# A decoder layer on one core: GpSimd adds before it reads back, pooling differences and norm splits issued sooner

## The chip, the cores and the metric

One NeuronCore of a Trainium2 chip runs the whole layer; nothing is exchanged with other cores. The metric is device time in microseconds. Engines are named as the profile names them: PE (TensorE), DVE (VectorE), ACT (ScalarE), POOL (GpSimd) and SP (SyncE). Each takes its instructions in program order and waits on semaphores. SP only issues transfers here; POOL computes and issues transfers from the same list.

## The reference, cut to what matters

All arrays are float32, with 256 tokens of width 1024. The part around the change is the first mixer and its norm:

```python
z = h @ w_in[l]                              # u | q | k | v, 512 columns each
pool_out = multiscale_pool(u, w_pool[l], pool_scale[l])
attn_out = moba_attention(q, k, v)           # 8 heads of 64; one block of 256, so causal softmax
mix = jnp.concatenate([pool_out, attn_out], axis=-1) @ w_out[l]
h = layer_norm(DEEPNORM_ALPHA * h + mix, ln1_g[l], ln1_b[l])
h = layer_norm(DEEPNORM_ALPHA * h + memory_cross_attention(h, mem, ...), ...)
h = layer_norm(DEEPNORM_ALPHA * h + swiglu(h, ...), ...)

# multiscale_pool, for the four groups g of 128 channels, windows w = 2, 4, 8, 16
groups.append((c_hi - c_lo) / count - uf[..., sl])   # trailing mean minus the token
mixed = einsum('bsgc,gcd->bsgd', pooled, w_pool)     # one 128x128 matrix for each group
```

## The kernel before, in words

Every large product is made of three float32r matmuls: each operand is split into a high part (a cast on ACT) and a low part (a subtraction on DVE), and PE adds high by high, high by low and low by high. The weights stream in through SP: `w12r` is piece number 12 as it lands, `w12h` and `w12l` its two parts. The splits of weight pieces are slipped into the program while PE works on earlier pieces, nine pieces ahead.

The program is written out by hand. Generators such as `do_u`, `do_xk` and `do_xv` yield after every few matmuls, and `run(u, 4)` advances one by four steps; what stands between two `run` calls is issued between those steps, on whichever engine it belongs to. The stages that matter here, in order:

- `do_u` projects u into `upad` in two chunks of 16 steps. When the first step of the second chunk is asked for, the first chunk is copied to `upad` by ACT (line 621) and `windows(0)` and `windows(1)` are issued: POOL adds shifted copies (line 593: one add for group 0, two for group 1, three for 2, four for 3) and corrects the first 16 tokens (line 595). At the end of the second chunk the same happens for groups 2 and 3.
- `scores` makes the softmax of four attention heads and one half of the tokens. `probs_out(hp)` turns two heads' probabilities on DVE (line 425, four 32x32 transposes a call) and sends them to HBM from POOL's queue (line 428, `pd<-ps`). `probs_in(hp)` reads them back transposed with four transfers from POOL's queue (line 436, `pt<-pd`), which wait until the transfer out has landed. `attend(hp)` is the product with v on PE (lines 581 and 582).
- `pool_diff(g)` is one DVE instruction (line 600) that subtracts the token from the window's mean, in `upad`. `mix_pool(g)` is the group's product on PE (line 604), with its split on ACT and DVE (lines 605 and 606).
- `do_xk` projects the memory's keys for the cross-attention in 64 steps, as PE's work between all this. Then comes the mix with w_out, norm 1, and `do_xv` (values of the memory) as PE's work while norm 1's result `h1` goes to HBM and back through SP's queue (`hr<-hd`).
- `h1_split(t)` splits half t of the result that came back, `hr`, into `h1Th` on ACT and `h1Tl` on DVE (lines 404 and 405). The projection `do_xq`, which follows `do_xv` on PE, reads both, and `xscores` reads its result `xq`.

Of the kernel before, what the change touches and what calls it, by code (L numbers as in the profile page):

```python
# [42 lines left out]
class Stream:  # L43
# [114 lines left out]
    def next(self):  # L158

        i = len(self.tiles)  # L160
        return i + (2 if i < len(self.items) and self.items[i][0] == "sums" else 1)
# [28 lines left out]
def decoder_layer(  # L190
# [105 lines left out]
    def split_mem(k):  # L296
        split(mT[0][:, k:k + 4, :], mT[1][:, k:k + 4, :], mr[0][:, k:k + 4, :])
# [97 lines left out]
    def run(gen, n=None):  # L395

        while n is None or n > 0:
            if next(gen, gen) is gen:
                return False
            n = None if n is None else n - 1  # L400
        return True
# [18 lines left out]
    def turned(blocks, n, name, queue=nc.sync):  # L420

        st = sp.tile([P, 4, n, 32], F32, name=f"{name}s", tag="pair", bufs=3)
        for at, src in blocks:
            m = src.shape[1]
            nc.vector.transpose(st[:, :, at:at + m, :].rearrange("p j m b -> p m j b"),  # L425
                                src.rearrange("p m (j b) -> p m j b", b=32))
        via = hp.tile([P, 4, n * 32], F32, name=f"{name}d")
        queue.dma_start(via, st.rearrange("p j m b -> p j (m b)"))  # L428
        return via
# [101 lines left out]
    def scores(hq, t):  # L531
        w = (t + 1) * P
        pss = [bank(f"ps{j}").rearrange("p (h s) -> p h s", h=2) for j in range(2)]
        for h in range(2):
            for j in range(2):
                hs = slice(j * HD, (j + 1) * HD)
                hp = 2 * hq + h
                nc.tensor.matmul(pss[j][:, h, :w], qT[hs, hp, t * P:(t + 1) * P], kT[hs, hp, :w],
                                 start=True, stop=True)
        todo = []  # L540
        for j in range(2):
            pr = sp.tile([P, 2, S], F32, name="pr", bufs=PR_BUFS)[:, :, :w]
            mx = sp.tile([P, 2], F32, name="mx", bufs=6)
            for h in range(2):
                nc.vector.tensor_tensor_reduce(pr[:, h, :], pss[j][:, h, :w], tri[:, S - w:], -1.0, -NEG,  # L545
                                               op0=OP.add, op1=OP.min, accum_out=mx[:, h:h + 1])
            todo.append((pr, exps(pr, pr, mx, -1.0)))
            probs[hq, t, j] = pr
        for pr, sm in todo:
            scaled(pr, sm)  # L550
# [6 lines left out]
    def probs_out(hp):  # L557
        blocks = []
        for j in range(2):
            for t in range(T):  # L560
                pr = probs[hp // 2, t, j][:, hp % 2]
                blocks.append((3 * j + t, pr.rearrange("p (m c) -> p m c", c=P)))
        turns[hp] = turned(blocks, 6, "p", nc.gpsimd)

    def probs_in(hp):
        if hp % 2 == 0:
            homes[hp // 2] = ap.tile([P, 2, KD * P], F32, tag="a8", name=f"pt{hp // 2}")
        raw = homes[hp // 2][:, hp % 2, :4 * 6 * 32].rearrange("p (i m b) -> p i m b", i=4, m=6)
        raw = landed(turns[hp], 6, "p", nc.gpsimd, raw).rearrange("p i m b -> p m i b")
        pts[hp] = [(raw[:, 3 * j:3 * j + 2], raw[:, 3 * j + 2]) for j in range(2)]  # L570
# [3 lines left out]
    def attend(hp):  # L574
        po = bank("po")
        for j in range(2):
            hs = slice(j * HD, (j + 1) * HD)
            vs = slice((2 * hp + j) * HD, (2 * hp + j + 1) * HD)
            s0, s1 = pts[hp][j]
            out = po[hs, :S].rearrange("p (t i b) -> p t i b", t=T, i=4)  # L580
            nc.tensor.matmul(out, vt[:, 0, vs], s0, start=True, stop=False)
            nc.tensor.matmul(out[:, 1], vt[:, 1, vs], s1, start=False, stop=True)
        split(cT[0][:, 4 + hp, :], cT[1][:, 4 + hp, :], po[:, :S])
# [14 lines left out]
    def pool_diff(g):  # L598
        pl = upad[:, g, PADW:]
        nc.vector.scalar_tensor_tensor(pl, sums[g][:, PADW:], 1.0 / WINDOWS[g], pl, op0=OP.mult, op1=OP.subtract)  # L600

    def mix_pool(g):
        pm = bank("pm")
        nc.tensor.matmul(pm[:, :S], wpl[:, g, :], upad[:, g, PADW:], start=True, stop=True)
        nc.scalar.activation(cT[0][:, g, :], pm[:, :S], AF.Copy, bias=0.0, scale=psc[:, g:g + 1])
        nc.vector.scalar_tensor_tensor(cT[1][:, g, :], pm[:, :S], psc[:, g:g + 1],
                                       r32(cT[0][:, g, :]), op0=OP.mult, op1=OP.subtract)


    def do_v():  # L610
        pieces = [(t, 0, 512) for t in range(T)]
        acc = {piece: accbank("pv") for piece in pieces}
        yield from proj_rows(acc, c_v, lambda k: (xT[0][:, k], xT[1][:, k]), pieces, True, True, True)
        for piece in pieces:
            nc.scalar.copy(vt[:, piece[0], :], acc[piece])

    def do_u():
        for c in range(2):
            ps = accbank("pu").rearrange("p (f t) -> p f t", f=2)
            yield from proj_t([ps[:, f, :] for f in range(2)], c_u[c], xT)  # L620
            nc.scalar.copy(upad[:, 2 * c:2 * c + 2, PADW:], ps)
            for f in range(2):
                windows(2 * c + f)
# [3 lines left out]
    def do_xk():  # L627
        for c in range(4):
            ps = accbank("pxk").rearrange("p (f t) -> p f t", f=2)
            yield from proj_t([ps[:, f, :] for f in range(2)], c_xk[c], mT)  # L630
            split(xkT[0][:, 2 * c:2 * c + 2, :], xkT[1][:, 2 * c:2 * c + 2, :], ps)

    v, u, xk = do_v(), do_u(), do_xk()
# [8 lines left out]
    probs_out(1)  # L642
    run(u, 6)
    split_mem(0)
    run(u, 4)
    probs_in(0)
    probs_in(1)
    run(u, 6)
    split_mem(4)
    run(u)  # L650
    run(xk, 2)
# [3 lines left out]
    run(xk, 8)  # L655
    scores(1, 1)
    run(xk, 8)
    probs_out(2)
    probs_out(3)
    mix_pool(0)  # L660
    attend(0)
    run(xk, 6)
    mix_pool(1)
    pool_diff(2)
    probs_in(2)
    probs_in(3)
    run(xk, 8)
    attend(1)
    pool_diff(3)
    ws.pace = 2  # L670
    run(xk, 8)
    mix_pool(2)
# [94 lines left out]
    def h1_split(t):  # L767
        raw = turns1[t].rearrange("p i k b -> p k i b")
        for k0 in (0, 4):
            h, l = [h[:, k0:k0 + 4, t * P:(t + 1) * P].rearrange("p k (i b) -> p k i b", i=4) for h in h1T]  # L770
            split(h, l, raw[:, k0:k0 + 4])
# [23 lines left out]
    def do_xv():  # L795
        acc = {piece: (bank if piece == PIECES[3] else accbank)("xv") for piece in PIECES}
        yield from proj_rows(acc, c_xv, lambda k: (mT[0][:, k], mT[1][:, k]),
                             PIECES, True, True, True)
        for t, c0, c1 in PIECES:
            split(xv[0][:, t, c0:c1], xv[1][:, t, c0:c1], acc[t, c0, c1])  # L800

    gv = do_xv()
    run(gv, 7)
    h1_split(0)
    run(gv, 5)
    h1_split(1)
    run(gv)

# [430 lines left out]
```

## Time and profile before

| | us |
|---|---|
| median of three runs | 372.5 |
| lowest and highest of them | 371.69 and 373.01 |
| the profiled execution, whole time | 372.51 |
| its span, from the first to the last instruction | 370.7 |

The profiled execution stands at the median, and 1.81 us of it lie outside the span. The granted TensorE clock is 0.998 of full speed over the span. In the rows below a start is in us from the span's start; the second number of a timeline row is its duration, and what stands in brackets is the idle time of that engine just before the row with what ended it.

### The profile page before, as it was taken

How to read it: one execution, taken by the hardware profiler on the slowest of the kernel's cores; microseconds unless marked ns; L12 is line 12 of the kernel's file. 1: busy time of each engine (PE TensorE's matmuls, PEld its weight loads, DVE VectorE, ACT ScalarE, POOL GpSimd, SP SyncE). 2: the span in 40 equal slices, each digit the busy share in tenths (PEclk: the TensorE clock that was granted, in tenths of full speed). 3: DMA queues.
4: the chain of work that ended last, by engine and by line, in shares of the span. 5: the costliest groups of instructions: out<-in, count | busy, mean ns of one | idle time of the engine just before them, and what ended most of it. 6: DMA issues, size and time to landing. Idle time of an engine off the chain costs nothing.

```text
span 370.7 us, 5690 instructions
## 1 busy us (share of the span) xinstructions
PE 362.7 (98%) x2007; PEld 312.7 (84%) x2007; DVE 301.6 (81%) x449; ACT 193.3 (52%) x289; POOL 59.2 (16%) x94
## 2 busy tenths in 40 slices
PE   8999999999999999999999999999999999999994
PEld 8997998897888899988878888888888888888882
DVE  5777898984599797765889897999999995789864
ACT  5656865753253565554229363754655555577000
POOL 1000059140020003320100042402321400000010
PEclk9999999999999999999999999999999999999999
DMA  7997599799615996846106998669887977758011
GB/s 244 416 422 286 187 338 303 272 280 362 214 66 173 357 356 234 277 149 207 57 2 191 400 273 262 212 204 361 271 290 254 315 260 245 232 166 260 9 57 58
DMA packets 33550, 88.21 MB, mean 238 GB/s; under 512 B 4209, under 2 KB 12401, under 8 KB 33393
## 3 DMA queue, kind: packets, MB, share of 16 engines
q1 hardware_dynamic: 31232, 82.66, 65.1%
q0 software_dynamic: 1712, 4.72, 4.0%
q10 hardware_dynamic: 576, 0.46, 0.4%
q8 instruction: 16, 0.26, 0.3%
q14 instruction: 14, 0.11, 0.1%
HBM read 80.48 MB, written 7.34 MB: 237 GB/s over the span
## 4 chain that ended last, share of the span: by engine, by line
PE 71%; issue 13%; DVE 6%; DMA 4%; POOL 3%; ACT 1%; SPq 0%; DVEq 0%; POOLq 0%; ACTq 0%
PE pg L343 10%; PE pg L342 10%; PE pg L341 10%; PE pqk L477 6%; PE acc L341 5%; PE acc L342 5%; PE acc L343 5%; PE pxk L359 2%; PE x L342 2%; PE x L343 2%; PE x L341 2%; PE acc L1121 1%; PE acc L1122 1%; PE acc L1120 1%; DMA pd<-ps 1%
## 5 line engine op out<-in xcount | busy, mean ns | idle before, releaser
L708 POOL TENSOR_TENSOR rs<-rs,mhalf 128x1 f32<-128x1 f32 x6 | 5.5, 910 | 128.2 <-DVE rs L707 128.2
L939 POOL TENSOR_TENSOR sraw<-gr 128x128 f32<-128x128 f32 x7 | 7.1, 1018 | 76.7 <-DMA gr<-gd 63.4
L1181 ACT ACTIVATE diag<-ident,rs 128x128 f32<-128x128 f32 x1 | 0.4, 402 | 22.0 <-POOL rs L708 22.0
L514 ACT ACTIVATE pr<-pr,mx 128x128 f32<-128x128 f32 (+1 forms) x16 | 7.1, 446 | 8.6 <-DVE mx L545 8.6
L919 ACT ACTIVATE sg<-pg 128x256 f32<-128x256 f32 x22 | 8.2, 381 | 6.4 <-PE pg L343 6.3
L428 POOL DMA_DIRECT2D pd<-ps x4 | 2.4, 612 | 48.5 <-DVE ps L425 48.2
L436 POOL DMA_DIRECT2D pt<-pd x16 | 8.8, 555 | 6.9 <-DMA pd<-ps 4.2
L920 DVE TENSOR_TENSOR sg<-sg,pg 128x256 f32<-128x256 f32 x22 | 8.6, 415 | 1.2 <-ACT sg L919 0.9
L404 ACT CAST h2Th<-tp 128x512 fp32r<-128x512 f32 x4 | 2.4, 588 | 13.5 <-PE tp L415 13.4
L405 DVE TENSOR_TENSOR gTl<-gr,gTh 128x512 fp32r<-128x512 f32 x11 | 8.0, 731 | 0.5 <-ACT gTh L404 0.5
L436 POOL DMA_DIRECT2D xr<-xd x12 | 6.5, 551 | 9.8 <-DMA xd<-xs 5.7
L404 ACT CAST gTh<-gr 128x512 fp32r<-128x512 f32 x11 | 6.8, 614 | 2.5 <-DMA gr<-gd 2.5
L514 ACT ACTIVATE xpr<-xs,mx 128x256 f32<-128x256 f32 x8 | 3.7, 471 | 8.1 <-DVE mx L525 8.1
L425 DVE STREAM_TRANSPOSE gs<-sg 128x512 f32<-128x512 f32 x11 | 7.7, 703 | 0.0
L428 POOL DMA_DIRECT2D xd<-xs x3 | 1.7, 576 | 33.8 <-DVE xs L425 33.8
L700 DVE BATCH_NORM_STATS2 st<-r 128x6 f32<-128x512 f32 (+1 forms) x10 | 6.4, 641 | 0.3
L940 POOL TENSOR_TENSOR sraw<-sraw,gr 128x128 f32<-128x128 f32 x7 | 6.5, 927 | 0.5
L519 DVE RECIPROCAL sm<-sm 128x2 f32<-128x2 f32 x12 | 2.0, 164 | 5.5 <-ACT xpr L514 4.4
L521 DVE TENSOR_SCALAR pr<-pr,sm 128x128 f32<-128x128 f32 (+1 forms) x16 | 6.2, 428 | 0.3
L713 DVE SCALAR_TENSOR_TENSOR r<-r,mv,g 128x512 f32<-128x512 f32 x9 | 6.4, 744 | 0.0
L941 POOL TENSOR_TENSOR sraw<-gr 128x128 f32<-128x128 f32 x7 | 6.1, 868 | 0.0
L719 DVE SCALAR_TENSOR_TENSOR h<-r,rs,b 128x512 f32<-128x512 f32 x8 | 5.6, 746 | 0.0
(1329 smaller groups left out, 1490.2 us busy)
## 6 DMA issues: line engine op xcount, KB each, us to landing
gd<-gs SPq DMA_DIRECT2D x11, 256.0 KB, 5.2
gr<-gd SPq DMA_DIRECT2D x44, 64.0 KB, 2.3
pd<-ps POOLq DMA_DIRECT2D x4, 384.0 KB, 4.5
pt<-pd POOLq DMA_DIRECT2D x16, 96.0 KB, 7.0
g<-in_ln_g SPq DMA_DIRECT2D x3, 512.0 KB, 5.8
b<-in_ln_b SPq DMA_DIRECT2D x3, 512.0 KB, 6.6
wr<-in_w_qkv SPq DMA_DIRECT2D x5, 256.0 KB, 4.6
mr<-in_mem_t SPq DMA_DIRECT2D x1, 1024.0 KB, 11.9
```

Source lines behind the costliest of these rows:

```text
L341: nc.tensor.matmul(ps, wa, ya, start=start, stop=False, skip_group_check=part)
L342: nc.tensor.matmul(ps, wa, yb, start=False, stop=False, skip_group_check=part)
L343: nc.tensor.matmul(ps, wb, ya, start=False, stop=stop, skip_group_check=part)
L359: nc.tensor.matmul(pss[f], w[:, s], y, start=k == 0 and f == 0 and n == 0, stop=k == KD - 1 and n == 2, skip_group_check=True)
L404: nc.scalar.copy(h, ps)
L405: nc.vector.tensor_sub(l, ps, r32(h))
L425: nc.vector.transpose(st[:, :, at:at + m, :].rearrange("p j m b -> p m j b"), src.rearrange("p m (j b) -> p m j b", b=32))
L436: queue.dma_start(raw[32 * j:32 * (j + 1)].rearrange("p i m b -> p i (m b)"), via[:, j, :].rearrange("(i a) r -> a i r", i=4))
L477: nc.tensor.matmul(qk[i][:, f, :], w[:, c * P:(c + 1) * P], y, start=k == 0 and f == 0 and w is hi and y is x_hi, stop=k == KD - 1 and w i ...
L514: nc.scalar.activation(dst[:, j, :], src[:, j, :], AF.Exp, bias=mx[:, j:j + 1], scale=sign, accum_out=sm[:, j:j + 1])
L919: nc.scalar.activation(sg, ps[:, :CW].rearrange("p (f b) -> p f b", f=2), AF.Silu, bias=0.0, scale=1.0)
L920: nc.vector.tensor_mul(sg, sg, ps[:, CW:].rearrange("p (f b) -> p f b", f=2))
```

## The change

Three things move; no instruction is added or taken away. First, `probs_in(0)` and `probs_in(1)` are issued after the first step of u's second chunk and no longer four steps ahead of the chunk's end, so that `windows(0)` and `windows(1)` stand ahead of them. Second, `pool_diff(2)` stands ahead of `probs_out(2)`, and `pool_diff(3)` where `pool_diff(2)` stood. Third, `h1_split(0)` comes after 6 steps of `do_xv` in place of 7, and `h1_split(1)` after 10 in place of 12.

```diff
     split_mem(0)
-    run(u, 4)
+    run(u, 10)
     probs_in(0)
     probs_in(1)
-    run(u, 6)
     split_mem(4)
...
     scores(1, 1)
     run(xk, 8)
+    pool_diff(2)
     probs_out(2)
     probs_out(3)
     mix_pool(0)
     attend(0)
     run(xk, 6)
     mix_pool(1)
-    pool_diff(2)
+    pool_diff(3)
     probs_in(2)
     probs_in(3)
     run(xk, 8)
     attend(1)
-    pool_diff(3)
...
     gv = do_xv()
-    run(gv, 7)
+    run(gv, 6)
     h1_split(0)
-    run(gv, 5)
+    run(gv, 4)
     h1_split(1)
     run(gv)
```

POOL's list from the transfer out of heads 0 to 3 (`pd<-ps`, one row for both) to the third group's sums, before:

```order
L428 DMA pd<-ps 128x768 x2
L436 DMA pt_641<-pd 32x4x192 x8
L593 TENSOR_TENSOR win<-upad 128x271
L595 TENSOR_TENSOR win<-win,fac 128x16
L593 TENSOR_TENSOR win<-upad 128x271
L593 TENSOR_TENSOR win<-win 128x269
L595 TENSOR_TENSOR win<-win,fac 128x16
L593 TENSOR_TENSOR win<-upad 128x271
```

The same stretch of POOL's list with the change:

```order
L428 DMA pd<-ps 128x768 x2
L593 TENSOR_TENSOR win<-upad 128x271
L595 TENSOR_TENSOR win<-win,fac 128x16
L593 TENSOR_TENSOR win<-upad 128x271
L593 TENSOR_TENSOR win<-win 128x269
L595 TENSOR_TENSOR win<-win,fac 128x16
L436 DMA pt_675<-pd 32x4x192 x8
L593 TENSOR_TENSOR win<-upad 128x271
```

The five instructions of groups 0 and 1 now stand ahead of the eight read-backs (four for heads 0 and 1, then four for heads 2 and 3).

On DVE, around the transposes of `probs_out(2)`, the difference of the third group (`upad<-win,upad`) comes in ahead of the first transpose:

```order
 L405 TENSOR_TENSOR xkTl<-pxk,xkTh 128x512
 L143 TENSOR_TENSOR w27l<-w27r,w27h 128x1024
+L600 SCALAR_TENSOR_TENSOR upad<-win,upad 128x256
 L425 STREAM_TRANSPOSE ps<-pr 128x4x32
 L425 STREAM_TRANSPOSE ps<-pr 128x2x4x32
```

It stood 12 rows further down, behind eight transposes, two splits of products, the split of w28 and one more product split; that place is now the fourth group's.

On ACT, in the middle of `do_xv` (`w44h` to `w49h` are casts of weights for the projection xq, `h1Th` the casts of norm 1's result, two for each half):

```order
 L142 CAST w44h<-w44r 128x1024
 L142 CAST w45h<-w45r 128x1024
+L404 CAST h1Th<-hr 128x4x128 x2
 L142 CAST w46h<-w46r 128x1024
+L142 CAST w47h<-w47r 128x1024
 L404 CAST h1Th<-hr 128x4x128 x2
-L142 CAST w47h<-w47r 128x1024
 L142 CAST w48h<-w48r 128x1024
-L404 CAST h1Th<-hr 128x4x128 x2
 L142 CAST w49h<-w49r 128x1024
```

Each half's casts are one weight piece sooner, and DVE's subtractions move in the same way.

## Rows read from the trace of the kernel before

**Rows 1.** The page, busy time of each engine over the span.

```profile
PE 362.7 (98%) x2007; PEld 312.7 (84%) x2007; DVE 301.6 (81%) x449; ACT 193.3 (52%) x289; POOL 59.2 (16%) x94
```

**Rows 2.** Waits of PE: total us, times, longest.

```profile
PE pm L604 <- DVE upad L600: 0.7, 1, 0.7
...
PE xs L343 <- DVE xq L409: 0.2, 1, 0.2
```

**Rows 3.** Timeline of PE, around the third and the fourth group's product.

```profile
71.92 0.28 PE L359 MATMUL pxk<-mTh,w23l 128*128 128x256 f32 x1
...
73.48 0.28 PE L359 MATMUL pxk<-mTl,w24h 128*128 128x256 f32 x1
...
77.54 0.28 PE L359 MATMUL pxk<-mTh,w25l 128*128 128x256 f32 x1
...
78.22 0.28 PE L359 MATMUL pxk<-mTl,w25h 128*128 128x256 f32 x1
```

**Rows 4.** Timeline of PE, scores of the cross-attention's first and second head.

```profile
135.86 0.28 PE L342 MATMUL xs<-xkTl,xq 128*128 128x256 f32 x1
...
136.57 0.28 PE L341 MATMUL xs<-xkTh,xq 128*128 128x256 f32 x1
...
143.52 0.28 PE L342 MATMUL xs<-xkTl,xq 128*128 128x256 f32 x1
...
143.76 0.28 PE L341 MATMUL xs<-xkTh,xq 128*128 128x256 f32 x1
```

**Rows 5.** Timeline of DVE, from the memory's splits to the third group's difference.

```profile
47.30 1.22 DVE L405 TENSOR_TENSOR mTl<-mr,mTh 128x1024 fp32r<-128x1024 f32 x1
...
52.97 1.22 DVE L143 TENSOR_TENSOR w24l<-w24r,w24h 128x1024 fp32r<-128x1024 f32 x1
...
56.67 0.86 DVE L521 TENSOR_SCALAR pr<-pr,sm 128x128 f32<-128x128 f32 x2
...
58.69 0.85 DVE L600 SCALAR_TENSOR_TENSOR upad<-win,upad 128x256 f32<-128x256 f32 x1 [0.83 <-POOL win L595]
59.46 1.65 DVE L143 TENSOR_TENSOR w25l<-w25r,w25h 128x1024 fp32r<-128x1024 f32 x1
...
67.97 2.18 DVE L425 STREAM_TRANSPOSE ps<-pr 128x128 f32<-128x128 f32 x8
...
72.30 0.41 DVE L600 SCALAR_TENSOR_TENSOR upad<-win,upad 128x256 f32<-128x256 f32 x1
```

**Rows 6.** Timeline of POOL, the read-backs and the sums.

```profile
51.39 4.38 POOL L436 DMA_DIRECT2D pt<-pd  x8 [4.25 <-DMA pd<-ps]
55.79 0.68 POOL L593 TENSOR_TENSOR win<-upad 128x271 f32<-128x271 f32 x1
...
58.44 0.22 POOL L595 TENSOR_TENSOR win<-win,fac 128x16 f32<-128x16 f32 x1
...
64.81 0.22 POOL L595 TENSOR_TENSOR win<-win,fac 128x16 f32<-128x16 f32 x1
```

**Rows 7.** Timeline of POOL, the read-backs of heads 4 to 7.

```profile
73.67 4.37 POOL L436 DMA_DIRECT2D pt<-pd  x8 [2.66 <-PE pm L604]
```

**Rows 8.** Timeline of DVE, ahead of the projection xq.

```profile
126.33 1.23 DVE L143 TENSOR_TENSOR w48l<-w48r,w48h 128x1024 fp32r<-128x1024 f32 x1 [0.62 <-ACT w48h L142]
127.47 1.29 DVE L405 TENSOR_TENSOR h1Tl<-hr,h1Th 128x512 fp32r<-128x512 f32 x2
```

**Rows 9.** Timeline of ACT, the first chunk of u.

```profile
47.13 0.59 ACT L621 COPY upad<-pu 128x512 f32<-128x512 f32 x1 [1.38 <-PE pu L359]
```

**Rows 10.** Timeline of POOL, one add of the third group's sums.

```profile
60.11 1.49 POOL L593 TENSOR_TENSOR win<-win 128x265 f32<-128x265 f32 x1
```

**Rows 11.** Timeline of PE, the first product with v, attend(0).

```profile
61.78 0.66 PE L581 MATMUL po<-pt,vt 128*64 128x256 f32 x4
```

**Rows 12.** Transfers: fourth read-back of probs_in(0), then of probs_in(2); us to landing.

```profile
pt<-pd POOLq DMA_DIRECT2D x1, 96.0 KB, 7.8
...
pt<-pd POOLq DMA_DIRECT2D x1, 96.0 KB, 5.3
```

## The prediction

> **What bounds the kernel now.** I read the page first: PE is busy for 362.7 of 370.7 us [rows 1]. With so little idle time the change can gain only what PE waits at the places that it touches, and lose only what it makes PE wait anew. So the second view was the waits of PE. Two of them lie where the change works: the third group's product waits 0.7 us for its pooling difference on DVE, and the scores of the cross-attention's first head wait 0.2 us for `xq` [rows 2]. Everything between and behind runs at PE's own pace, so what PE gains or loses at 62, 72 or 136 us is carried to the end.
>
> Third came the timelines, for the true price of a wait, because a matmul that follows a stop also starts slowly. From the last projection matmul ahead of `mix_pool(2)` to the second one behind it go 73.48 - 71.92 = 1.56 us; around `mix_pool(3)`, which has the same instructions and no wait, 78.22 - 77.54 = 0.68 us [rows 3]. The wait costs 0.88 us. For the scores, 136.57 - 135.86 = 0.71 us stand against 143.76 - 143.52 = 0.24 us one head later [rows 4], so up to 0.47 us.
>
> **The change, part by part.**
>
> *The pooling differences.* `pool_diff(2)` ran at 72.30 us and moves ahead of transposes that began at 67.97 us [rows 5], some four microseconds ahead of PE's need at 72 us. Its input is ready: all sums were finished at 65.03 us [rows 6], and the third group's before that. So mix_pool(2) no longer waits: **-0.88 us**, as long as nothing else is late there. It puts 0.41 us of DVE ahead of the transposes and takes it from behind them. `pool_diff(3)` takes the place at 72.30, five us ahead of its product, which follows the 77.54 row [rows 3, 5]. Both cost nothing, and without that cover at most 0.41 us each. The transposes' transfers and their read-backs shift by that 0.41 at most; the late read-backs start at 73.67 [rows 7] for products of the next stage.
>
> *Norm 1's splits.* The second half's subtraction ran at 127.47 us behind w48's, whose cast made DVE wait 0.62 us [rows 8]. Now it stands ahead of w48 and can use that gap. DVE then comes to `xq` sooner by 0 to 0.62 us, and PE's wait there is worth 0 to 0.47 us. I take **-0.2 us**, a little under the middle, because the next casts wait for weights in the same way and give part of the gap back. The first half moves ahead of one weight piece, w46, which belongs to the second head's projection: nothing.
>
> *The sums ahead of the read-backs.* This is the part that can cost. What is gained directly is DVE's 0.83 us wait at 58.69 for the second group's sums [rows 5], which no PE instruction sees. What is paid is on POOL. Before, eight read-backs went out from 51.39 us, and the two groups' five instructions followed from 55.79 to 58.66 [rows 6], when DVE had small work. Now the five run first. The chunk of u is in `upad` at 47.13 + 0.59 = 47.72 us [rows 9]. At their old pace, 2.87 us, they would end at 50.6, ahead of the read-backs' own wait for `pd`, and the delay would be zero: the lower bound.
>
> But from 47.30 to 54.19 DVE runs two-input subtractions back to back, one each (52.97 - 47.30)/5 = 1.13 us [rows 5]. Where the trace has a POOL add beside such a subtraction, both stretch: w25's took 1.65 us where the others take 1.22 [rows 5], and the add took 1.49 us [rows 10] where one beside small work took 0.68 [rows 6]. They read as taking turns: the add sits until DVE's instruction is through, and DVE's next one starts 0.43 us late. With that the first add ends at about 49.05, and each further POOL instruction ends one subtraction later: a correction 1.13 us later, an add 1.13 + 0.43 = 1.56 us later. That gives 50.2, 51.75, 53.3 and 54.45 us. The read-backs start at 54.5, which is **3.1 us late**. DVE itself loses three times 0.43, 1.3 us, there, and has it back by about 60 us, since the same turns and the 0.83 us wait are gone later.
>
> Who waits for the read-backs? `attend(0)`, at 61.78 us [rows 11], for the first four. Their issues are 0.55 us apart (4.38 / 8), so the fourth went out at 53.04 and landed 7.8 us later, at 60.84 [rows 6, 12]: 0.94 us of slack, against 3.1 us of delay. Counted from the first issue that was 9.45 us. The later four (73.67 + 1.64 + 5.3 = 80.6) took 6.95 us [rows 12, 7]. From 54.5 these two give landings at 63.95 and 61.45, so PE waits between 2.2 us and nothing. I take 8.4 us, somewhat nearer the first batch, which met the same weight traffic: landing 62.9, **+1.1 us**. The other four are wanted 14 of the 64 steps of the keys' projection later and have more room; the third and fourth groups' sums start about as before, at 59.
>
> One rule could raise this. The trace shows eight issues of 0.55 us each while DVE's subtractions run, the same as in the later batch [rows 6, 7], so the issue itself is not held. The Trainium skill, page "SBUF — State Buffer", section "SBUF: two separate sides", says that a transfer issued by GpSimd has its descriptors written by GpSimd's cores, which are locked out of SBUF while DVE runs certain instructions. If that holds here, the landing and not the issue stretches; it is the third case below.
>
> *Sum.* 372.51 (the profiled execution, at the median of the runs) - 0.88 - 0.2 + 1.1 = 372.5 us.
>
> **The rivals.** About 0.3%, 1.1 us, is what a measurement of this kernel tells from no change; the bounds are 371.4 and 373.6.
>
> 1. *A new wait at attend(0) eats the gain* (the forecast, 0.55). Waits of 0.3 to 2.2 us: 371.7 to 373.6. For it: the stretched pair at 59 to 61 us. Against it: the turns are read from one stretch and carried to another.
> 2. *The read-backs are in time* (0.25). Either POOL isn't held up, or with fewer transfers beside them they land as fast as the late batch. Then 372.51 - 0.88 - (0 to 0.47) = 371.2 to 371.6. For it: the late batch's 6.95 us puts the landing at 61.45, ahead of 61.78.
> 3. *Slower* (0.16): the descriptors are held up by DVE. From 54.5 to 59 DVE now runs the softmax's scalings, two pairs of 0.86 us as in the row at 56.67 [rows 5], 1.7 us that the read-backs would have to sit out. Landing 62.9 + 1.7 = 64.6, wait 2.8 us, 372.51 + 2.8 - 0.88 - 0.2 = 374.2. For it: the first batch was the slower one. Against it: the issues were not stretched. It decides from a landing at 64.0 us, where the wait passes 2.2.
> 4. *The change doesn't act* (0.04): the third difference is held by its sums and PE waits as before, 372.5. The sums' end, 65.03 against a need at 68, speaks against it.
>
> **How the numbers follow.** The time is that of the first case. The range reaches from the lower end of the second case, 371.2, to 374.0, which leaves out the greater part of the third; the first case alone gives 371.7 to 373.6. Faster by over 0.3%: somewhat over half of the second case, 0.15. Slower: the third case and the upper edge of the first, 0.2. The same: 0.65.
>
> **What would show it.** Right: PE's wait for `upad` at mix_pool(2) is gone from the list of waits, and one at `po` for `pt<-pd` has come, of about 1 us; the first five POOL instructions take some 6.7 us in place of 2.87, and the first read-back goes out near 54.5. Wrong: read-backs at 51.4 (no turns), or no wait at `po` (case 2), or a fourth read-back landing after 64 (case 3). The norm's step is right if DVE's 0.62 us gap ahead of w48 has gone and the wait at `xs` has shrunk. What would make the whole wrong is a wait of PE in a place that I have not named, such as a late weight piece in the stretch from 55 to 75 us, where DVE is 1.3 us behind for a while.

## The result, and the profile after

The changed kernel takes 373.78 us (median of nine runs, 373.17 to 376.01) against 372.12 us of the kernel before on the same chip: a ratio of 1.0053 with a 95% interval of 1.0037 to 1.0068. (The ratios here are estimates of their own and not exactly quotients of the medians, which give 1.0045.) It is slower by half a per cent, where no change was forecast; 373.78 lies inside the range given. The profiled execution is one of the shorter ones, 373.17 us with a span of 371.3, against 372.51 and 370.7 before.

PE's waits after, which answer to [rows 2] (us in total, times, longest):

```profile
PE po L581 <- DMA pt<-pd: 2.1, 1, 2.1
PE out L1183 <- ACT diag L1180: 1.4, 1, 1.4
PE busy L448 <- PEq L1202: 0.8, 1, 0.8
PE tp L415 <- DVE h L718: 0.4, 1, 0.4
```

The wait of `pm` for `upad` and the one of `xs` for `xq` have gone from the list, and one at `attend(0)` has come. The timeline of PE shows what each is worth: at the first product with v, around the third group's product, and at the first cross-attention scores, which answer to [rows 11, 3, 4].

```profile
61.05 0.60 PE L604 MATMUL pm<-upad,wpl 128*128 128x256 f32 x2
63.72 0.66 PE L581 MATMUL po<-pt,vt 128*64 128x256 f32 x4 [2.07 <-DMA pt<-pd]
64.17 0.42 PE L582 MATMUL po<-pt,vt 128*64 128x128 f32 x4
64.53 0.39 PE L359 MATMUL pxk<-mTh,w21h 128*128 128x256 f32 x1
...
73.84 0.28 PE L359 MATMUL pxk<-mTh,w23l 128*128 128x256 f32 x1
...
74.52 0.28 PE L359 MATMUL pxk<-mTl,w24h 128*128 128x256 f32 x1
...
136.85 0.28 PE L342 MATMUL xs<-xkTl,xq 128*128 128x256 f32 x1
...
137.40 0.28 PE L341 MATMUL xs<-xkTh,xq 128*128 128x256 f32 x1
```

Around `mix_pool(2)` now 74.52 - 73.84 = 0.68 us, the price without a wait, so the 0.88 us are gained. At the scores 137.40 - 136.85 = 0.55 us in place of 0.71: 0.16 us gained. At `attend(0)` PE stands for 2.07 us.

The timeline of POOL after, from the first group's add to the read-backs, answers to [rows 6]:

```profile
47.66 1.14 POOL L593 TENSOR_TENSOR win<-upad 128x271 f32<-128x271 f32 x1 [0.72 <-ACT upad L621]
48.88 1.08 POOL L595 TENSOR_TENSOR win<-win,fac 128x16 f32<-128x16 f32 x1
49.93 1.61 POOL L593 TENSOR_TENSOR win<-upad 128x271 f32<-128x271 f32 x1
51.62 1.50 POOL L593 TENSOR_TENSOR win<-win 128x269 f32<-128x269 f32 x1
53.20 1.08 POOL L595 TENSOR_TENSOR win<-win,fac 128x16 f32<-128x16 f32 x1
54.23 4.41 POOL L436 DMA_DIRECT2D pt<-pd  x8
```

Five instructions that took 2.87 us take 6.57, from 47.66 to 54.23, and the read-backs go out 2.84 us later than before. DVE's timeline after, [rows 5] and [rows 8], has the other side of it, three subtractions of 1.65 us and more beside POOL's adds, and then the third group's difference and norm 1's split in their new places:

```profile
48.22 1.66 DVE L143 TENSOR_TENSOR w21l<-w21r,w21h 128x1024 fp32r<-128x1024 f32 x1
49.81 1.24 DVE L405 TENSOR_TENSOR mTl<-mr,mTh 128x1024 fp32r<-128x1024 f32 x1
50.97 1.66 DVE L143 TENSOR_TENSOR w22l<-w22r,w22h 128x1024 fp32r<-128x1024 f32 x1
52.55 1.65 DVE L143 TENSOR_TENSOR w23l<-w23r,w23h 128x1024 fp32r<-128x1024 f32 x1
...
67.66 0.41 DVE L600 SCALAR_TENSOR_TENSOR upad<-win,upad 128x256 f32<-128x256 f32 x1
...
126.56 1.29 DVE L405 TENSOR_TENSOR h1Tl<-hr,h1Th 128x512 fp32r<-128x512 f32 x2
127.77 1.22 DVE L143 TENSOR_TENSOR w48l<-w48r,w48h 128x1024 fp32r<-128x1024 f32 x1
129.44 1.22 DVE L143 TENSOR_TENSOR w49l<-w49r,w49h 128x1024 fp32r<-128x1024 f32 x1 [0.46 <-ACT w49h L142]
```

DVE's gap of 0.62 us ahead of w48 is used; a gap of 0.46 us comes one piece later, as the prediction allowed for.

The fourth read-back, which `attend(0)` needs, took 7.7 us from its issue to its landing, against 7.8 before [rows 12]:

```profile
pt<-pd POOLq DMA_DIRECT2D x1, 96.0 KB, 7.7
```

With issues 0.55 us apart it landed at 54.23 + 1.65 + 7.7 = 63.58 us, 9.35 us after the first issue, and PE went on 0.14 us later. Before it was 9.45 us. So in these two profiles the read-backs took as long as before and were issued 2.84 us later.

What the read-backs meet has changed too. SP's queue of transfers, before and then after:

```profile
51.95 0.33 SPq L120 DMA_DIRECT2D w29r<-in_w_out  x1
52.33 0.43 SPq L277 DMA_DIRECT2D xt<-in_x  x1
53.09 0.33 SPq L120 DMA_DIRECT2D w30r<-in_w_out  x1
```

```profile
52.65 0.33 SPq L120 DMA_DIRECT2D w29r<-in_w_out  x1
53.03 0.43 SPq L277 DMA_DIRECT2D xt<-in_x  x1
54.23 0.34 SPq L120 DMA_DIRECT2D w30r<-in_w_out  x1
```

Before, the first read-back (51.39) was issued ahead of `w29r`, a weight piece of 512 KB, and of the tokens, `xt`, of 1024 KB. Now both go out ahead of it.

### The profile page after: what moved, and what is told of

It reads as the page before. It is cut to its first block, busy times and chain, and to the rows that moved or that the text cites. A ratio compares the mean times of both kernels' runs of the same rounds, so it can differ in the third digit from the quotient of the medians.

```text
span 371.3 us, 5688 instructions
## 1 busy us (share of the span) xinstructions
PE 362.6 (98%) x2007; PEld 313.1 (84%) x2007; DVE 302.2 (81%) x449; ACT 193.4 (52%) x289; POOL 62.2 (17%) x94
## 4 chain that ended last, share of the span: by engine, by line
PE 92%; DMA 2%; POOL 2%; DVE 2%; issue 1%; ACT 0%; DVEq 0%; POOLq 0%
PE pg L343 10%; PE pg L341 10%; PE pg L342 10%; PE pqk L477 6%; PE pxq L359 6%; PE acc L341 6%; PE acc L342 6%; PE acc L343 6%; PE pxk L359 5%; DMA pt<-pd 2%; PE xv L342 2%; PE xv L343 2%; PE xv L341 2%; PE x L343 2%; PE x L341 2%; PE x L342 2%
## 5 line engine op out<-in xcount | busy, mean ns | idle before, releaser
L938 POOL TENSOR_TENSOR sraw<-gr 128x128 f32<-128x128 f32 x7 | 5.3, 756 | 78.4 <-DMA gr<-gd 69.8
L593 POOL TENSOR_TENSOR win<-win 128x269 f32<-128x269 f32 (+2 forms) x6 | 5.6, 940 | 0.5
```

## The experiments

The theory after the result (**A**): the whole loss is at `attend(0)`; POOL's sums make the read-backs late, and there they share the DMA engines with weights and tokens that are issued ahead of them. The rival (**B**): the read-backs' descriptors are held up by DVE. Two further rivals came up on the way: that DVE's lost 1.3 us is what costs, and that the longer runs have nothing to do with PE's stop. "Low clock" counts the runs whose mean granted clock was 0.994 or less; the kernel before has none in the 99 runs beside the experiments (0.995 to 1.000). The wait is that of one profiled execution each.

| run | median us | ratio to before, 95% interval | PE's wait at `attend(0)`, us | low clock |
|---|---|---|---|---|
| the change | 373.78 | 1.0053 [1.0037, 1.0068] | 2.1 | 1 of 9 |
| the change again | 375.86 | 1.0087 [1.0055, 1.0119] | 3.2 | 4 of 7 |
| sums only | 375.5 | 1.0067 [1.0043, 1.0091] | 2.2 | 7 of 12 |
| without the sums' move | 371.37 | 0.9971 [0.9959, 0.9983] | none | 0 of 12 |
| differences only | 372.06 | 0.9978 [0.9964, 0.9992] | none | 0 of 12 |
| norm splits only | 372.43 | 0.9997 [0.9981, 1.0013] | 0.8 | 0 of 12 |
| tokens later | 374.31 | 1.0038 [1.0017, 1.0058] | 1.6 | 4 of 12 |
| one group ahead | 371.62 | 0.9946 [0.9926, 0.9966] | none | 0 of 6 |
| scores later | 375.73 | 1.0071 [1.0051, 1.0091] | 2.5 | 5 of 6 |
| `attend(0)` later | 372.31 | 0.9979 [0.9964, 0.9995] | 0.4 | 0 of 12 |
| PE busy, 2 us of zeros | 374.71 | 1.0072 [1.0047, 1.0097] | 0.4 | 2 of 12 |
| PE busy, 3.6 us of zeros | 374.84 | 1.0054 [1.0035, 1.0073] | none | 0 of 6 |
| PE busy, 3.4 us of data | 374.74 | 1.0058 [1.0042, 1.0074] | none | 0 of 6 |
| without the sums' move, tokens later | 372.0 | 0.999 [0.9977, 1.0002] | none | 0 of 12 |
| one group ahead, tokens later | 371.57 | 0.9974 [0.996, 0.9989] | none | 0 of 12 |

**The parts apart.** Four runs, against the kernel before.

Sums only:

```diff
-    run(u, 4)
+    run(u, 10)
     probs_in(0)
     probs_in(1)
-    run(u, 6)
```

> The sums of groups 0 and 1 ahead of the read-backs and nothing else of the change. Theory (the loss is a late read-back at attend(0)): the wait at po is there as with the whole change, about 2 us, and the whole time is 1.0 to 2.0 us above the kernel before, since a PE that is 2 us late at attend(0) no longer waits at the third group's product, so that the difference's old place costs nothing here. Rival (the loss comes from the moved difference or the norm's splits): within 0.4 us of the kernel before.

The wait came as expected, 2.2 us, and the kernel is slower by more than the wait and more than expected: 2.5 us by the ratio. The windows of its profiled execution, one with a low clock, show why (busy time of each engine, then PEclk, the granted clock):

```profile
60.00:64.50 4.50, 2.35 (x18) 1.98 (x18) 4.30 (x14) 3.04 (x10) 4.11 (x6) 1.00 1.03 284
64.50:68.00 3.50, 3.50 (x17) 2.95 (x18) 3.50 (x5) 2.98 (x5) 2.12 (x3) 0.52 0.87 238
68.00:70.00 2.00, 2.00 (x16) 1.95 (x16) 2.00 (x8) 0.26 (x1) 0.20 (x1) 0.99 0.85 272
```

PE had stood 2.15 us until 64.50, and for the next 3.5 us the granted clock was 0.52, nearly all of it at the lower level, 1.2 GHz. The matmuls follow each other at 0.21 us there, as in these two rows of PE's timeline, in place of 0.12:

```profile
66.73 0.41 PE L359 MATMUL pxk<-mTh,w21h 128*128 128x256 f32 x1
66.94 0.41 PE L359 MATMUL pxk<-mTl,w21h 128*128 128x256 f32 x1
```

The same work from `po` on, to the start of the tenth matmul of the projection behind it, takes 68.01 - 64.50 = 3.51 us there and 65.69 - 63.72 = 1.97 us in the profiled execution of the change, which kept its clock: 1.5 us lost behind the stop. The Trainium skill, page "TensorE: Matmul & The Clock Gate", section "HAM oscillation — how this bites in real kernels", says that a wait for a transfer can put the clock back so that the work behind it starts slowly; this trace agrees, with 0.52. In the profile of the change the clock behind the stop of 2.07 us was 1.00.

Without the sums' move (parts two and three):

```diff
+    pool_diff(2)
     probs_out(2)
...
-    pool_diff(2)
+    pool_diff(3)
...
-    pool_diff(3)
...
-    run(gv, 7)
+    run(gv, 6)
     h1_split(0)
-    run(gv, 5)
+    run(gv, 4)
```

> The difference moved and the norm's splits sooner, without the sums ahead of the read-backs. Theory: no wait at po, none at the third group's product: 0.9 to 1.3 us below the kernel before. Rival: no faster than the kernel before, because the moved instructions bring a wait of their own.

Differences only, the first four changed lines of that:

> The two pooling differences moved and nothing else. Theory: the 0.88 us at the third group's product go, 0.7 to 0.9 us below the kernel before. Rival (the PE comes sooner and waits for the norm or the scores instead): less than 0.4 us below.

Norm splits only, its last four:

> Norm 1's splits two steps sooner and nothing else. Theory: 0 to 0.3 us below the kernel before, by a shorter wait at the scores; DVE's gap ahead of w48 goes. Rival (the casts wait for the transfer and hold the weights up): 0.2 us or more above it.

So the first part alone costs what the change costs and more, and the other two gain 1.1 us (0.9971 of 372.5). The differences gain 0.8 us of it. The norm's splits alone can't be told from nothing, and in that run's profile the wait at the first head's scores was 0.36 us, longer than the 0.21 before. In the same profile the read-backs, in their old place and issued at 51.58 us, were late by 0.8 us: the slack of 0.94 us that the prediction read was not there in every execution.

**What holds the read-backs: A or B.** Both edits are of the changed kernel. The tokens later:

```diff
-    ws.before(c_mix[3][0], load_x)
+    ws.before(c_mix[7][0], load_x)
```

> The changed kernel, with the 1 MB load of the tokens (xt), which stood among the hardware queue's transfers of 52 to 64 us, moved behind a later group of weights. In the changed kernel the first data of the read-backs moved 3.8 us after the first issue (2.1 in the kernel before) and TensorE stood 2.07 us at attend(0). Theory A (the read-backs share the DMA engines with the weights and tokens queued ahead of them): the lag falls to about 2 us, the wait at attend(0) to 0.5 us or less, and the time to 371.6 (371.0 to 372.3). Theory B (the read-backs' descriptors are written late because VectorE's two-input subtractions hold them up): the lag stays at 3.8 us, the wait near 2.1 and the time near 373.7.

The scores later, so that DVE's work beside the issue is another:

```diff
     run(xk, 2)
-    scores(1, 0)
     pool_diff(0)
     pool_diff(1)
-    run(xk, 8)
+    run(xk, 4)
+    scores(1, 0)
+    run(xk, 4)
```

> The changed kernel, with the scores of the next heads four steps of the token projection later, so that VectorE's work at 54 to 58 us, while GpSimd issues the read-backs, is another. Theory A (DMA engines shared with the hardware queue): the lag from first issue to first data stays near 3.8 us and the wait at attend(0) near 2 us; time 373.7 (372.8 to 374.6). Theory B (descriptors held up by VectorE): the lag falls towards 2.1 us, the wait to 0.5 us or less, time 371.8.

The transfers in the four microseconds from the first read-back's issue on: packets, MB, and their time as a share of 16 engines. First the change (from 54.23 us; q0 is POOL's queue, q1 the one of SP), then the tokens later (54.21), then the scores later (54.99):

```profile
q1 hardware_dynamic: 399, 1.51, 100.0%
q0 software_dynamic: 2, 0.01, 0.6%
```

```profile
q1 hardware_dynamic: 245, 0.91, 79.1%
q0 software_dynamic: 48, 0.11, 10.9%
```

```profile
q1 hardware_dynamic: 393, 1.49, 97.9%
q0 software_dynamic: 3, 0.01, 0.7%
```

In the change the DMA engines are full with SP's transfers, and the read-backs move two packets in four microseconds. Without the tokens among those, 48 packets get through in the same time, although DVE and POOL do the same work at the same times, to 0.03 us. That speaks for A and against B as what holds back the start. The scores-later run, meant to decide between them, doesn't: in its four microseconds DVE ran the subtractions of w24 and w25 and two differences (54.88 to 57.93 us), no less than beside the change. It does show that the scalings of the prediction's third case are not needed for a late start: they ran from 59.28 us on, and the read-backs still moved 3 packets.

For the time the start matters less than A says. With the tokens later the wait fell to 1.6 us only and not to the 0.5 expected, and the ratio of 1.0038 can't be told from the change's: the issue is as late as before, and two more weight pieces share the engines. Ten batches, with the landing reckoned as above, show how loosely it follows SP's traffic:

| run | first issue, us | SP's MB in the 4 us from it | fourth landing, us after the first issue |
|---|---|---|---|
| the kernel before | 51.39 | 1.13 | 9.4 |
| its later heads | 73.67 | 0.93 | 6.9 |
| the change | 54.23 | 1.51 | 9.4 |
| the change again | 54.34 | 1.42 | 10.5 |
| scores later | 54.99 | 1.49 | 9.7 |
| tokens later | 54.21 | 0.91 | 8.9 |
| without the sums' move | 49.80 | 0.95 | 7.1 |
| differences only | 50.00 | 0.97 | 9.4 |
| norm splits only | 51.58 | 1.22 | 10.6 |
| one group ahead, tokens later | 50.72 | 0.91 | 6.8 |

Between 0.91 and 0.97 MB the landing lies anywhere from 6.8 to 9.4 us, so this traffic does not tell it. What sets the change apart from the kernel before is the time of the issue; without the tokens the landing is half a microsecond shorter (8.85 against 9.35 us), which is less than two executions of the change differ by, so what the tokens cost is not shown.

The profile puts the wait of the scores-later run, 2.5 us, down to a scaling on DVE that ended at 64.84 us. That scaling is of heads 4 to 7, which `attend(0)` doesn't read; the fourth read-back landed at 64.65, and in the other profiles with a stop PE goes on 0.1 to 0.2 us after that landing, as here (64.86). So it is taken as the same read-back. The Trainium skill, page "SBUF — State Buffer", section "SBUF: two separate sides", has a GpSimd instruction that reads SBUF and a DVE instruction with two inputs there lock each other out for the whole of one of them. For POOL's own sums the trace agrees (a correction of 0.22 us takes 1.08, a subtraction of 1.22 us takes 1.66); that it delays the read-backs' descriptors, no run here shows.

**Is it the time of issue?** One group's sums ahead of the read-backs, the other's behind:

```diff
-            for f in range(2):
+            for f in range(1 if c == 0 else 2):
                 windows(2 * c + f)
...
     probs_in(1)
+    windows(1)
```

> The changed kernel, but GpSimd forms the pooling sums of one group only ahead of the read-backs (two additions and one multiplication fewer), and the other group's behind their issue. Theory A (the wait at attend(0) follows the time of the first issue): the read-backs are issued near 51.4 us in place of 54.2, the wait falls to 0 to 0.8 us as in the run of parts two and three alone and of part three alone, and the time to 371.6 (371.0 to 372.6). Rival (any sums ahead of the read-backs cost the whole wait, because something else holds the transfers until 58 us): wait 1.5 us or more and a time of 373 or more.

The first four read-backs go out at 51.31 us, as this row of POOL shows, and PE goes through `attend(0)` without a stop:

```profile
51.31 2.25 POOL L436 DMA_DIRECT2D pt<-pd  x4 [0.57 <-DMA pd<-ps]
```

Now they wait for the transfer out, not for the sums. The ratio of 0.9946 is the lowest of all, but the medians, 371.62 against 372.81 us, give 0.9968, no better than without the sums' move (371.37 against 372.59), and with the tokens later the ratio was 0.9974. So the loss is gone; a gain from the one group's move is not shown.

**Is it PE's stop, or what DVE and POOL lose?** The changed kernel, with other PE work ahead of the product:

```diff
     mix_pool(0)
-    attend(0)
     run(xk, 6)
+    attend(0)
```

> The changed kernel, with six steps of the token projection ahead of attend(0) in place of behind it, so that TensorE has some 4 us of other work while the read-backs land. GpSimd's five sums, the read-backs' issue at 54 us and VectorE's slower subtractions stay as in the changed kernel. Theory A (the loss is TensorE's stop at attend(0), and what its clock does behind it): no wait there, granted clock 1.00 throughout, and a time of 371.5 (371.0 to 372.2), like parts two and three alone (371.4). Rival (the loss is VectorE's 1.3 us of slower subtractions, or GpSimd's later work): the time stays at 373 or more though the wait is gone.

POOL's sums, the issue (54.39 us) and DVE's slower subtractions are as in the change; only PE has something to do. PE's row:

```profile
64.35 0.66 PE L581 MATMUL po<-pt,vt 128*64 128x256 f32 x4 [0.41 <-DMA pt<-pd]
```

The ratio is 0.9979, and no run of twelve has a low clock; on the same chip four of twelve runs with the tokens later had one, and five of six with the scores later. So the loss is PE's stop with what follows from it; the 1.3 us of DVE cost nothing that shows. The 372.31 us are 0.1 over the upper end of what was expected, but the kernel before ran 0.3 us longer in that comparison too.

**Two sizes of the loss.** The change once more:

> The changed kernel once more, beside the next run on the same chip. Its wait at attend(0) again 1.8 to 2.5 us, time 1.004 to 1.007 of the kernel before. If TensorE's clock is what makes some runs longer, the runs of 375 us and more are those with a granted clock of 0.992 to 0.995, and the runs of 373 to 374 those with 0.997 and above.

Its profiled execution, with the same instructions, stood longer:

```profile
65.00 0.66 PE L581 MATMUL po<-pt,vt 128*64 128x256 f32 x4 [3.24 <-DMA pt<-pd]
```

Both the stop and the ratio, 1.0087, lie above what was expected. The fourth read-back took 8.8 us to land in place of 7.7, so the landing differs by over a microsecond between executions of one kernel. This longer stop was not followed by a low clock (1.00 from 65.00 to 68.50 us), so the length of the stop alone doesn't decide that. Of the 16 timed runs of the change, the five at 0.994 or less took 375.69 to 378.19 us with 375.89 in the middle, the other eleven 373.17 to 376.01 with 373.78 in the middle. Three runs fill the stop, each ahead of `attend(0)` in the changed kernel. Nine multiplications of zeros, and then sixteen:

```diff
     mix_pool(0)
+    keep_busy(9)
     attend(0)
```

> The changed kernel, with nine multiplications of zeros ahead of attend(0) (0.22 us each by the eighteen at the kernel's start, so 2.0 us in all), whose result nothing reads: TensorE works where it stood, and attend(0) starts no sooner. If the stop costs its own length and in some runs a half-speed stretch behind it, the length stays and the half speed goes: no run below a granted clock of 0.997, none above 374.8 us, median 373.3 (1.002 to 1.004 of the kernel before). Rival (the longer runs have nothing to do with TensorE's stop): the same spread as the changed kernel, with runs of 375 us and more.

> The changed kernel, with sixteen multiplications of zeros ahead of attend(0), whose result nothing reads: 16 by 0.22 us make 3.6 us, more than the longest stop seen there (3.2 us), so that TensorE has no stop at all, and attend(0) starts 0.4 to 1.5 us later than in most runs of the changed kernel. If half-speed stretches come from the stop, no run is below a granted clock of 0.995 and none above 376 us, median about 374.7 (the changed kernel's 373.2 at full clock and 1.5 us). Rival (multiplying zeros is no better than standing, or the long runs come from elsewhere): runs of 0.992 to 0.994 and above 376 us remain, as with the nine multiplications.

And eight products with data:

```diff
     mix_pool(0)
+    again = bank("again")
+    for _ in range(8):
+        nc.tensor.matmul(again[:, :S], wpl[:, 0, :], upad[:, 0, PADW:], start=True, stop=True)
     attend(0)
```

> The changed kernel, with the pooling mix's first multiplication done eight more times into a tile that nothing reads, ahead of attend(0): 3.4 us of TensorE work with data that are not zeros, in the place of the stop. If half-speed stretches come from TensorE's standing (or multiplying zeros), no run is below a granted clock of 0.995 and none above 375.5 us, median about 374.6. If they come whatever TensorE does there, the same share of runs at 0.992 to 0.994 remains.

The nine did not do what was expected: two of twelve runs still had a low clock, the longest 378.26 us, and three without one took more than the 374.8 us expected, up to 377.35. So the clock is not the whole of the spread. They fill 2.17 us and left a stop of 0.36 us in the profile; a landing as late as the 3.24 above would leave over a microsecond. With the stop filled whole, by zeros or by data, no run of six and six has a low clock, and the times are close together, 373.94 to 375.46 and 374.63 to 375.0, at the medians expected to 0.2 us. So the low clock goes with PE's standing, not with late data by itself, though it doesn't follow every stop. (The change was not run beside these twelve, and `attend(0)` starts later in them, so they are strong evidence and not proof.)

**The later tokens by themselves.** The same line as above, in the kernel without the sums' move and in the one with one group ahead:

> Parts two and three alone, with the load of the tokens later. Parts two and three alone had no wait at attend(0), so there is nothing for the later load to take away: 0.997 of the kernel before (0.9955 to 0.9985), about 371.4 us. If the later load costs or gives something of its own, it shows here, and has to be taken from what it gave the changed kernel.

> The changed kernel with one group's sums ahead of the read-backs, and the load of the tokens later. One group ahead alone had no wait at attend(0) and 0.9946 of the kernel before; the later load should leave that as it is: 0.995 (0.9935 to 0.9975), no wait at attend(0).

Neither gains by it. The ratios are 0.2 and 0.3% above those without the later load; the intervals touch, and the medians of the second pair hardly differ, so a cost is not shown for certain. The profile of the first has a place for one: the tokens now go out at 66.98 us, ahead of the later heads' transfers, whose read-backs are issued at 76.62 in place of 73.67 us, and PE stops for 0.41 us at a product of those heads (87.65 us). The ratio, 0.999, lies outside what was expected. In part this cost may have hidden what the later load gave the change above.

## Why the prediction was wrong, point by point

- **What bounds the kernel** held: PE lost at 62 us and gained at 72 and 136 us, and each was carried to the end, as the sum below shows.
- **The pooling differences**, -0.88 us: right in the trace to the hundredth; alone 0.8 us in the times.
- **Norm 1's splits**, -0.2 us: 0.16 us in the trace; too small for the times to show alone. In three other profiles with the splits moved (norm splits only, tokens later, 3.6 us of zeros) the wait at the first head's scores was 0.28 to 0.36 us against 0.21 before, so that the move shortens it is not shown.
- **The sums' pace on POOL**: right, and so was the taking of turns with DVE. Read-backs at 54.5 us were foretold, 54.23 came; 6.7 us for the five instructions, 6.57 came. What DVE loses cost nothing, as said.
- **The wait at `attend(0)`**, +1.1 us: this step failed. The mechanism was right and its size was not. The prediction took 8.4 us from the first issue to the fourth landing, between the first batch's 9.45 and the late batch's 6.95. It was 9.35, the first batch's own figure, within a tenth. That alone moved the landing from the forecast 62.9 to 63.58 us, although the issue came 0.27 us sooner than forecast. PE reached the product 0.21 us sooner than before and went on 0.14 us after the landing, which make up the rest: in place of +1.1 the term was 2.07 us of idle time in one profiled execution, 2.15 from product to product, and 3.24 of idle time in another. The late batch's row, 6.95 us, gave no ground for a shorter landing: the ten landings above lie between 6.8 and 10.6 us, and the four of them that follow all five sums at 8.85 or more. The slack of 0.94 us was read from one execution too, and in another, with the read-backs in their old place, there was none.
- **The clock** was not in the sum. In some executions PE runs at the lower level behind its stop: for some 3.5 us, at 1.5 us more, in the profiles of sums only and of scores later. Of the change no profile has it; 5 of its 16 timed runs have the low mean clock that goes with it.
- **The rivals.** The third was near in size (wait 2.8 us, 374.2 us), but the runs don't bear out its mechanism: with the scalings moved to 59.28 us and later the read-backs started as late as they did, and with DVE's work unchanged and the tokens gone they started sooner. The second, read-backs in time, is what the run with one group ahead shows.

With the measured terms the sum is 372.51 - 0.88 - 0.16 + 2.15 = 373.62 us, against 373.17 of the profiled execution. Laid beside each other product by product, the two profiles show the other 0.45 us, outside the places that the three terms price. PE is 0.21 us ahead since the first weights, as at the product ahead of `attend(0)` (61.26 before, 61.05 after); it gains 0.06 us at the start of the projection xq, and 0.18 us at the scores of a later head, where the kernel before has a gap of 0.39 us between these rows and the changed kernel, below it, one of 0.21:

```profile
157.56 0.28 PE L342 MATMUL xs<-xkTl,xq 128*128 128x256 f32 x1
157.95 0.39 PE L343 MATMUL xs<-xkTh,xq 128*128 128x256 f32 x1
```

```profile
158.40 0.28 PE L342 MATMUL xs<-xkTl,xq 128*128 128x256 f32 x1
158.61 0.39 PE L343 MATMUL xs<-xkTh,xq 128*128 128x256 f32 x1
```

From there to the end the difference stays at 0.66 us, which is 373.17 - 372.51. The median lies above that execution, by the longer landings and the clock.

Left open: why the landing differs by over a microsecond between executions of the same kernel, and why one stop of 2.15 us is followed by a low clock and one of 3.24 us is not. B was tested by the tokens-later run only; a run with fewer DVE subtractions beside the issue was not made. What in the DMA engines makes a full queue of SP hold back the start of POOL's transfers is open too; only the packets are known.

## What to carry to other kernels

When an issue of a transfer moves, look at what else it is moved past: not only its own queue and engine, but the transfers that another queue issues meanwhile. A landing time read from one row is one draw: here the same four read-backs took 6.8 to 10.6 us, so take the row of the same batch as the price, not a figure between two batches, and give the term that whole spread. And where the bound engine gets a new stop, price the work behind the stop too, from a run that shows it at the lower clock, and try half of the move: one group's sums ahead kept the gain of the other two parts and left the read-backs in time.

## What the runs showed that was not expected

- Eight read-backs of 96 KB moved 2 packets in four microseconds beside 1.51 MB of SP's queue at a share of 100.0%, and 48 beside 0.91 MB at 79.1%; yet the fourth landed only half a microsecond sooner.
- The same instructions gave a stop of 2.07 us in one profiled execution and of 3.24 in another.
- After a stop of 2.15 us the granted clock was 0.52 for 3.5 us, with matmuls 0.21 us apart in place of 0.12; filled with multiplications of zeros that nothing reads, the stop had no such consequence in six runs.
